# A decoder block in split fp32: scaled activations made by VectorE in wide pieces, w_up's halves added a tick later, the keys' transposes four ticks later

## The chip, the cores and the metric

The kernel runs on one core of a Trainium2 chip, as one program. The metric is the device time of one execution in microseconds (us). The engines are TensorE (PE in the profile; PEld is its weight load), VectorE (DVE), ScalarE (ACT), GpSimd (POOL) and SyncE (SP), which starts most of the transfers. Each engine works through its own instructions in the order in which the program holds them and waits on semaphores for what others produce.

## The reference

One layer of a decoder, in float32, for 256 tokens of width 1024:

```
h = rms_norm(x, norm_mix_g);  proj = h @ w_in            # u | q | k | v, 512 each
q, k = rope(rms_norm(q)), rope(rms_norm(k))              # 8 heads of 64
x = x + concat(pool_mixer(u), attention(q, k, v)) @ w_out
h = rms_norm(x, norm_xattn_g)
x = x + cross_attention(h, rms_norm(mem)) @ w_xo         # 4 heads of 256, 256 memory rows
h = rms_norm(x, norm_ffn_g)
up = causal_conv3(h @ w_up) + conv_b                     # 2 x 2816 channels
x = x + (silu(gate) * val) @ w_down                      # 2816 -> 1024
```

The outputs are the 256 x 1024 values of the last x.

## The kernel before

**Products in three passes.** TensorE takes operands in a rounded format (fp32r). Each fp32 operand is split into a high part h (rounded) and a low part l (the rest), and a product is h·h + h·l + l·h. Activations are split once per stage: ScalarE rounds (`part_h`, L253 and L255), VectorE subtracts (`part_l`, L259 and L261). A split activation tile lies as [h | l], 512 columns for 256 tokens.

**Weights.** All weights stream from HBM as chunks of 1 MB (`raw`), each two units of 1024 columns. For each unit ScalarE makes `wh` (L194) and VectorE `wl` (L205); `need(u)` puts both into the program at the point at which a unit is first asked for, some units ahead of its use.

**Matmuls.** The in-projection is made by `a_chunk` (L378 to L390), with the weights as the moving operand: for each of 8 blocks of the width, h and l of two token tiles against `wh`, then h against `wl`. All later projections are made by `b_tile` with `both` (L276 to L282): for each block of 128 inputs one matmul of `wh` against [h | l] (512 columns; L278 or L282) and one of `wl` against h (256 columns; L279 or L281). The halves of the bank, h and l products, are added afterwards. L278 and L279 are the first pair of a tile, so L278 marks where a tile opens.

**The order of the work.** The matmuls are written in their order. All other work (norms, rotations, transposes, softmax, the convolution) is written as generators, the jobs. `tick()`, called after every second block, advances each open job by one step, and the numbers in the WAIT lists say how many ticks a job lets pass before its next step. So these numbers fix where each instruction stands on each engine; at run time only semaphores decide when it runs.

**Keys and queries.** `rope` and `qk_job` rotate and normalize them: products with the rotation tables, a sum (L432), a sum of squares, an inverse root on GpSimd, for the keys a product with it (L453), then eight transposes on TensorE (L460) and copies by ScalarE. The in-projection of u runs beside this. WAIT_QK[1] is the wait before the keys' transposes, WAIT_QK[0] that before the queries'.

**w_up.** 22 pairs of tiles, gate and value, of 8 blocks each. The norm's factor for each token (`r2b`, made at L910 by `r2_job`) is not there when the stage begins. The first three pairs (i < SCALED) use unscaled activations and their result is multiplied by r2b (L934). The others use `hs2`: the same activations with the factor in them. Eight GpSimd products (L920) make them, eight ScalarE activations round them, eight VectorE operations (L261) subtract. After a pair's second tile `up_job` (L924 to L956) runs: for both halves ScalarE copies the l part out of the bank (L928) and VectorE adds the h part (L929); ScalarE starts the convolution (y, L938), VectorE adds its two other taps (L945, four operations), ScalarE takes silu (L949), VectorE multiplies gate and value (L951), and the result is rounded and subtracted (L253, L259) into `act`, one of 22 blocks of w_down's input.

**w_down.** Eight tiles of 22 blocks, L984 to L990. Before a block is used, `act_tile` lets that pair's job run to its end. Each tile's halves are added to the residual by two VectorE additions (L989), and the result goes out by DMA.

**The head.** Twenty small matmuls (L351) run while the first weights and tokens arrive; `first_splits` splits the activations and the first weights, block by block.

Of the kernel before, what the change touches and what calls it, by code (L numbers as in the profile page):

```python
# [18 lines left out]
S = 256  # L19
KT = D // P  # L20
# [19 lines left out]
WAIT_MEAN = [0]  # L40
WAIT_STAT = [2, 14, 8, 0, 0, 30]
WAIT_ROPE = [6, 6, 0]
WAIT_QK = [12, 12, 8, 25, 0, 2]
WAIT_V = [2, 10]
WAIT_MEM = [2, 2]
WAIT_SCORE = [5, 4, 0, 9, 1, 6]
# [3 lines left out]
WAIT_R1 = [6]  # L50
WAIT_X = [3, 0, 0, 0, 10, 0, 6, 13, 8]
WAIT_VALUE = [32]
WAIT_R2 = [6, 6, 1, 1, 0]
WAIT_LOW = [2]
WAIT_UP = [6, 2, 5, 7, 9, 8]
SCALED = 3
# [21 lines left out]
def block_kernel(ctx: ExitStack, tc: tile.TileContext, wpack: bass.AP, xpack: bass.AP, scal: bass.AP,  # L78
# [56 lines left out]
    def wait(n):  # L135
        for _ in range(n):
            yield
# [113 lines left out]
    def part_h(h, src, scale=None):  # L251
        if scale is None:
            act.copy(h, src)  # L253
        else:
            act.activation(h, src, AF.Copy, scale=scale)  # L255
# [12 lines left out]
    def three(o, stat, mov, start, stop):  # L268
# [2 lines left out]
        pe.matmul(o, stat[0], mov[1], start=False, stop=False)  # L271
        pe.matmul(o, stat[1], mov[0], start=False, stop=stop)  # L272

    def both(b, stat, mov, start, stop):

        n = mov.shape[1] // 2  # L276
        if start:
            pe.matmul(b, stat[0], mov, start=True, stop=False)  # L278
            pe.matmul(b[:, 0:n], stat[1], mov[:, 0:n], start=False, stop=False)  # L279
        else:  # L280
            pe.matmul(b[:, 0:n], stat[1], mov[:, 0:n], start=False, stop=False)  # L281
            pe.matmul(b, stat[0], mov, start=False, stop=stop)  # L282

    def col(t, c):
        return t[:, c:c + 1]
# [80 lines left out]

    def first_splits():
        for k in range(KT):
            part_h(xgv[0][:, k], resid[:, k], col(sc, C_GMIX + k))
            part_l(xgv[1][:, k], resid[:, k], xgv[0][:, k], col(sc, C_GMIX + k))  # L370
            r = slice(k % 2 * 512, k % 2 * 512 + 512)
            split_h(k // 2, r, dve.tensor_copy if k == 0 else act.copy)
            split_l(k // 2, r)
        next_split[0] = FIRST

# [2 lines left out]
    def a_chunk(u0, actv, bk):  # L378

        for k in range(KT):  # L380
            w = need(u0 + k // 2)
            wv = [t[:, (k % 2) * 512:(k % 2) * 512 + 512] for t in w]
            a = [[t[:, k, tt * P:(tt + 1) * P] for t in actv[:2]] for tt in range(TT)]
            for tt in range(TT):
                pe.matmul(bk[tt], a[tt][0], wv[0], start=k == 0, stop=False)  # L385
                pe.matmul(bk[tt], a[tt][1], wv[0], start=False, stop=False)  # L386
            tick()
            for tt in range(TT):
                pe.matmul(bk[tt], a[tt][0], wv[1], start=False, stop=k == KT - 1)  # L389
            tick()  # L390
# [330 lines left out]

    def b_tile(u0, f, blocks, b, mov):

        for k in range(blocks):
            i = f * blocks + k
            w = need(u0 + i // 8)
            wv = [t[:, (i % 8) * P:(i % 8 + 1) * P] for t in w]
            both(b, wv, mov(k), k == 0, k == blocks - 1)
            halves[0] += 1
            if halves[0] % 2 == 0 and k < blocks - 1:  # L730
                tick()
# [168 lines left out]
    def r2_job():  # L900

        yield from wait(WAIT_R2[0])
        v2 = yield from row_mean(acc2, "2")
        r2 = rsqrt(v2, TT, True)
        yield from wait(WAIT_R2[1])
        b = bank()
        for tt in range(TT):
            pe.matmul(b[:, tt * P:(tt + 1) * P], col(r2, tt).to_broadcast([P, P]), ident, start=True, stop=True)
        yield from wait(WAIT_R2[2])
        dve.tensor_copy(r2b, b[:, 0:S])  # L910
        r2_ready.append(True)
        yield from wait(WAIT_R2[3])
        prev = None
        for k in range(KT + 1):
            if prev is not None:
                part_h(hs2[0][:, k - 1], prev, col(sc, C_GFFN + k - 1))
                part_l(hs2[1][:, k - 1], prev, hs2[0][:, k - 1], col(sc, C_GFFN + k - 1))
            if k < KT:
                t = t1(f"hs{k}")
                pool.tensor_tensor(t, resid[:, k], r2b, op=ALU.mult)  # L920
                prev = t
            yield from wait(WAIT_R2[4])

    def up_job(i, bs, scaled):  # L924
        src = t2(f"up{i}")
        for g in range(2):
            half = src[:, g * S:(g + 1) * S]
            act.copy(half, bs[g][:, S:])  # L928
            dve.tensor_tensor(half, bs[g][:, 0:S], half, op=ALU.add)  # L929
        if not scaled:  # L930
            while not r2_ready:
                yield
            src2 = src.rearrange("p (g s) -> p g s", g=2)
            dve.tensor_tensor(src2, src2, r2b[:, None, :].to_broadcast([P, 2, S]), op=ALU.mult)  # L934
        y = t2(f"y{i}")
        for g in range(2):
            f = i + g * NFF
            act.activation(y[:, g * S:(g + 1) * S], src[:, g * S:(g + 1) * S], AF.Identity, bias=col(sc, C_CB + f),  # L938
                           scale=col(sc, C_CW + 2 * 2 * NFF + f))
        yield from wait(WAIT_UP[1])  # L940
        for j in (1, 2):
            for g in range(2):
                f = i + g * NFF
                uu, yy = src[:, g * S:(g + 1) * S], y[:, g * S:(g + 1) * S]
                dve.scalar_tensor_tensor(yy[:, j:], uu[:, :S - j], col(sc, C_CW + (2 - j) * 2 * NFF + f), yy[:, j:],  # L945
                                         op0=ALU.mult, op1=ALU.add)
        yield from wait(WAIT_UP[2])
        sg = t2(f"sg{i}")
        act.activation(sg[:, 0:S], y[:, 0:S], AF.Silu)  # L949
        yield from wait(WAIT_UP[3])  # L950
        dve.tensor_tensor(sg[:, S:], sg[:, 0:S], y[:, S:], op=ALU.mult)  # L951
        yield from wait(WAIT_UP[4])
        h, l = (t[:, i % 8] for t in acts[i // 8][:2])
        part_h(h, sg[:, S:])
        yield from wait(WAIT_UP[5])
        part_l(l, sg[:, S:], h)  # L956
# [2 lines left out]
    jobs_up = []  # L959
    look[0] = LOOKS[10]  # L960
    for i in range(NFF):
        bs = [bank(), bank()]
        if i == 0:
            hs2 = tiles(pair("hs2"), KT, S)
            job_r2.append(go(r2_job()))
        scaled = i >= SCALED
        hv = hs2 if scaled else h2
        if i == SCALED:
            finish(job_r2[0])
        for g in range(2):  # L970
            b_tile(58, 2 * i + g, KT, bs[g], lambda k: hv[2][:, k])
            if g == 0:
                tick()
        if i % 8 == 0:
            acts.append(tiles(pair(f"act{i // 8}"), KT, S))
        jobs_up.append(go(up_job(i, bs, scaled)))
        tick()

    def act_tile(k):
# [2 lines left out]

    look[0] = LOOKS[11]
    for f in range(KT):  # L984
        b = bank()
        b_tile(102, f, NFF, b, act_tile)
        o = t2(f"o{f}")[:, 0:S]
        for z, add in enumerate((resid[:, f], o)):
            dve.tensor_tensor(o, b[:, z * S:(z + 1) * S], add, op=ALU.add)  # L989
        nc.sync.dma_start(out[:, f], o)  # L990

# [98 lines left out]
```

## Time and profile before

| what | us |
|---|---|
| median of 3 runs | 391.47 |
| lowest, highest run | 390.37, 392.4 |
| the profiled execution: its time | 390.8 |
| the profiled execution: span from the first to the last instruction | 389.0 |
| PE busy | 381.3 (98% of the span) |
| DVE busy | 313.3 (81%) |
| ACT busy | 248.2 (64%) |
| POOL busy | 77.1 (20%) |

The span leaves out 1.8 us of the profiled execution's time that lie around it. Rows of a timeline give the start, the length, the engine, the line, the operation and out<-in; `x4` joins four neighbours, and a bracket gives the idle time before them and what ended it. The length of an instruction is longer than the distance to its neighbour's start, since neighbours overlap. Waits are given as total, times, longest. The granted TensorE clock is 1.000 over the whole execution.

### The profile page before, as it was taken

Reading aid. Unit: us, or ns where it says so; the run is one execution under the profiler, and the core shown is the slowest. Engines: PE = TensorE matmul, PEld = TensorE weight load, DVE = VectorE, ACT = ScalarE, POOL = GpSimd, SP = SyncE. Lnnn points to the kernel's source line nnn. Section 1 sums busy time; section 2 is a strip of 40 time slices with the busy share of each in tenths; the row PEclk is TensorE's granted clock in tenths of the full one; section 3 lists DMA queues with packets and bytes.
Section 4 is the critical chain, followed back from the end, with each engine's and each line's share of the span. In section 5 each row is a group of like instructions: output and inputs, shape, how many; then the busy total and the mean of one; then the engine's idle time right before and its main releaser. Section 6 shows DMA issues by size and latency. Waiting matters only on the chain.

```text
span 389.0 us, 5984 instructions
## 1 busy us (share of the span) xinstructions
PE 381.3 (98%) x2178; PEld 328.7 (84%) x2178; DVE 313.3 (81%) x562; ACT 248.2 (64%) x475; POOL 77.1 (20%) x160
## 2 busy tenths in 40 slices
PE   8999899999999999999999999999999999999995
PEld 8888688888888988898888878888888888888884
DVE  4769899978879859678978989999999998654460
ACT  5775797977557747745655678778877777442210
POOL 0272786142832122100325100000000000000000
PEclk9999999999999999999999999999999999999999
DMA  8985381453505624363535055555655554364400
GB/s 281 423 329 192 134 305 67 176 211 110 199 19 216 217 108 190 135 217 109 189 125 231 1 155 204 196 211 209 218 216 202 184 191 181 124 241 166 186 19 21
DMA packets 12269, 69.14 MB, mean 178 GB/s; under 512 B 1360, under 2 KB 2768, under 8 KB 4688
## 3 DMA queue, kind: packets, MB, share of 16 engines
q1 hardware_dynamic: 11952, 68.24, 47.5%
q10 hardware_dynamic: 288, 0.52, 0.4%
q8 instruction: 17, 0.28, 0.3%
q14 instruction: 12, 0.10, 0.1%
HBM read 67.71 MB, written 1.05 MB: 177 GB/s over the span
## 4 chain that ended last, share of the span: by engine, by line
PE 79%; DVE 9%; DMA 3%; ACT 3%; issue 2%; POOL 2%; SPq 0%; DVEq 0%
PE bank L282 34%; PE bank L281 17%; PE bank L385 5%; PE bank L386 5%; PE bank L389 5%; PE bank L278 4%; DVE wl L205 3%; PE bank L279 2%; DMA raw<-wpack 2%; DVE hs L261 2%; DMA sc<-xpack 1%; PE bank L272 1%; PE bank L271 1%; PE bank L270 1%; ACT wh L194 1%
## 5 line engine op out<-in xcount | busy, mean ns | idle before, releaser
L205 DVE TENSOR_TENSOR wl<-raw,wh 128x1024 fp32r<-128x1024 f32 (+1 forms) x126 | 149.3, 1202 | 3.1 <-ACT wh L194 3.1
L194 ACT CAST wh<-raw 128x1024 fp32r<-128x1024 f32 (+1 forms) x125 | 123.6, 1022 | 36.0 <-DMA raw<-wpack 35.0
L282 PE MATMUL bank<-hs,wh 128*128 128x512 f32 x266 | 94.8, 396 | 0.0
L281 PE MATMUL bank<-hs,wl 128*128 128x256 f32 x266 | 74.2, 279 | 0.0
L282 PE MATMUL bank<-act,wh 128*128 128x512 f32 x168 | 59.6, 398 | 0.0
L282 PEld LDWEIGHTS bank<-hs,wh 128*128 128x128 f32 x266 | 49.9, 188 | 10.3
L281 PEld LDWEIGHTS bank<-hs,wl 128*128 128x128 f32 x266 | 50.1, 189 | 1.6
L281 PE MATMUL bank<-act,wl 128*128 128x256 f32 x168 | 47.1, 281 | 0.0
L938 ACT ACTIVATE y<-up,sc 128x256 f32<-128x256 f32 x44 | 24.1, 595 | 27.0 <-DVE up L929 19.7
L282 PEld LDWEIGHTS bank<-act,wh 128*128 128x128 f32 x168 | 31.6, 188 | 7.4
L945 DVE SCALAR_TENSOR_TENSOR y<-up,sc,y 128x255 f32<-128x255 f32 (+1 forms) x88 | 36.6, 477 | 0.3 <-ACT y L938 0.3
L282 PE MATMUL bank<-h,wh 128*128 128x512 f32 x98 | 35.1, 396 | 0.0
L281 PEld LDWEIGHTS bank<-act,wl 128*128 128x128 f32 x168 | 31.7, 189 | 0.3
L281 PE MATMUL bank<-h,wl 128*128 128x256 f32 x98 | 27.6, 281 | 0.0
L989 DVE TENSOR_TENSOR o<-bank,sc 128x256 f32<-128x256 f32 x8 | 3.4, 425 | 29.4 <-PE bank L282 29.4
L385 PE MATMUL bank<-wh,mg 128*128 128x512 f32 x64 | 26.1, 408 | 0.0
L385 PE MATMUL bank<-wh,xg 128*128 128x512 f32 x64 | 26.0, 406 | 0.0
L386 PE MATMUL bank<-wh,xg 128*128 128x512 f32 x64 | 25.4, 397 | 0.0
L386 PE MATMUL bank<-wh,mg 128*128 128x512 f32 x64 | 25.1, 392 | 0.0
L747 POOL TENSOR_TENSOR h_acc<-h_sq,h_acc 128x256 f32<-128x256 f32 x14 | 13.4, 956 | 43.3 <-ACT h_sq L746 43.1
L282 PEld LDWEIGHTS bank<-h,wh 128*128 128x128 f32 x98 | 18.4, 188 | 3.6
L255 ACT ACTIVATE h<-sc 128x256 fp32r<-128x256 f32 x16 | 8.2, 511 | 20.5 <-DVE sc L739 20.4
(256 smaller groups left out, 770.1 us busy)
## 6 DMA issues: line engine op xcount, KB each, us to landing
raw<-wpack SPq DMA_DIRECT2D x59, 1024.0 KB, 4.8
raw<-wpack SPq DMA_DIRECT2D x4, 512.0 KB, 7.8
mraw<-memT SPq DMA_DIRECT2D x4, 256.0 KB, 6.8
out<-o SPq DMA_DIRECT2D x8, 128.0 KB, 1.9
raw<-wpack ACTq DMA_DIRECT2D x2, 256.0 KB, 3.5
raw<-wpack SPq DMA_DIRECT2D x2, 256.0 KB, 4.8
sc<-xpack SPq DMA_DIRECT2D x1, 512.0 KB, 6.4
tab<-table SPq DMA_DIRECT2D x1, 480.0 KB, 9.1
```

Source lines behind the costliest of these rows:

```text
L194: copy(split[u][0][:, r], unit(u)[:, r])
L205: dve.tensor_tensor(l[:, r], unit(u)[:, r], h[:, r].bitcast(F32), op=ALU.subtract)
L255: act.activation(h, src, AF.Copy, scale=scale)
L278: pe.matmul(b, stat[0], mov, start=True, stop=False)
L281: pe.matmul(b[:, 0:n], stat[1], mov[:, 0:n], start=False, stop=False)
L282: pe.matmul(b, stat[0], mov, start=False, stop=stop)
L385: pe.matmul(bk[tt], a[tt][0], wv[0], start=k == 0, stop=False)
L386: pe.matmul(bk[tt], a[tt][1], wv[0], start=False, stop=False)
L389: pe.matmul(bk[tt], a[tt][0], wv[1], start=False, stop=k == KT - 1)
L747: pool.tensor_tensor(acc, sq, acc, op=ALU.add)
L938: act.activation(y[:, g * S:(g + 1) * S], src[:, g * S:(g + 1) * S], AF.Identity, bias=col(sc, C_CB + f), scale=col(sc, C_CW + 2 * 2 * NFF ...
L945: dve.scalar_tensor_tensor(yy[:, j:], uu[:, :S - j], col(sc, C_CW + (2 - j) * 2 * NFF + f), yy[:, j:], op0=ALU.mult, op1=ALU.add)
```

## The change

Six things are changed.

- `r2_job`: VectorE makes the scaled activations (eight operations with gain and r2b at once, L922) instead of GpSimd; ScalarE rounds them in four pieces of 512 columns and VectorE subtracts in four pieces (L259). The waits there go from 1, 0 to 0, 1.
- The adding of a pair's halves leaves `up_job`. A new generator `up_half` is started after each tile: ScalarE copies at once, VectorE adds two ticks later (L932). `up_job` waits two ticks before its first step.
- WAIT_QK[1], ahead of the keys' transposes, goes from 12 to 16.
- `first_splits`: the cast of the first weights stands ahead of the first activations' subtraction.
- `a_chunk`: the h products of both token tiles come first, then the l products of both.
- The last tile of w_down uses `three` (three matmuls of 256 columns a block, summed in one bank half) and one addition.

```diff
-WAIT_QK = [12, 12, 8, 25, 0, 2]
+WAIT_QK = [12, 16, 8, 25, 0, 2]
...
-WAIT_R2 = [6, 6, 1, 1, 0]
+WAIT_R2 = [6, 6, 1, 0, 1]
...
+    def halves_of(t):
+        return [t[:, 0:S], t[:, S:]]
...
             part_h(xgv[0][:, k], resid[:, k], col(sc, C_GMIX + k))
+            split_h(k // 2, r, dve.tensor_copy if k == 0 else act.copy)
             part_l(xgv[1][:, k], resid[:, k], xgv[0][:, k], col(sc, C_GMIX + k))
-            split_h(k // 2, r, dve.tensor_copy if k == 0 else act.copy)
...
                 pe.matmul(bk[tt], a[tt][0], wv[0], start=k == 0, stop=False)
+            for tt in range(TT):
                 pe.matmul(bk[tt], a[tt][1], wv[0], start=False, stop=False)
...
+        product = both if b.shape[1] > S else three
...
-            both(b, wv, mov(k), k == 0, k == blocks - 1)
+            product(b, wv, mov(k), k == 0, k == blocks - 1)
...
-        prev = None
-        for k in range(KT + 1):
-            if prev is not None:
-                part_h(hs2[0][:, k - 1], prev, col(sc, C_GFFN + k - 1))
-                part_l(hs2[1][:, k - 1], prev, hs2[0][:, k - 1], col(sc, C_GFFN + k - 1))
-            if k < KT:
-                t = t1(f"hs{k}")
-                pool.tensor_tensor(t, resid[:, k], r2b, op=ALU.mult)
-                prev = t
-            yield from wait(WAIT_R2[4])
-
-    def up_job(i, bs, scaled):
-        src = t2(f"up{i}")
-        for g in range(2):
-            half = src[:, g * S:(g + 1) * S]
-            act.copy(half, bs[g][:, S:])
-            dve.tensor_tensor(half, bs[g][:, 0:S], half, op=ALU.add)
+        ts = []
+        for j in range(KT // 2):
+            ts.append(t2(f"hs{j}").rearrange("p (k s) -> p k s", k=2))
+            for k in range(2):
+                dve.scalar_tensor_tensor(ts[j][:, k], resid[:, 2 * j + k], col(sc, C_GFFN + 2 * j + k), r2b,
+                                         op0=ALU.mult, op1=ALU.mult)
+            part_h(hs2[0][:, 2 * j:2 * j + 2], ts[j])
+        yield from wait(WAIT_R2[4])
+        for j in range(KT // 2):
+            part_l(hs2[1][:, 2 * j:2 * j + 2], ts[j], hs2[0][:, 2 * j:2 * j + 2])
+
+    def up_half(o, b):
+        act.copy(o, b[:, S:])
+        yield from wait(WAIT_LOW[0])
+        dve.tensor_tensor(o, b[:, 0:S], o, op=ALU.add)
+
+    def up_job(i, src, scaled):
+        yield from wait(WAIT_LOW[0])
...
-        bs = [bank(), bank()]
+        up = t2(f"up{i}")
...
-            b_tile(58, 2 * i + g, KT, bs[g], lambda k: hv[2][:, k])
+            b = bank()
+            b_tile(58, 2 * i + g, KT, b, lambda k: hv[2][:, k])
+            go(up_half(up[:, g * S:(g + 1) * S], b))
...
-        jobs_up.append(go(up_job(i, bs, scaled)))
+        jobs_up.append(go(up_job(i, up, scaled)))
...
-        b = bank()
-        b_tile(102, f, NFF, b, act_tile)
+        last = f == KT - 1
+        b = bank()[:, 0:S] if last else bank()
+        b_tile(102, f, NFF, b, (lambda k: halves_of(act_tile(k))) if last else act_tile)
...
-        for z, add in enumerate((resid[:, f], o)):
+        for z, add in enumerate((resid[:, f], o)[:1 if last else 2]):
```

The order on VectorE in the steady part of w_up, before: the work of pair 5 (`up5`, `y5`), with older pairs' products (`sg4`) and subtractions (from `sg2`) between. Rows give line, operation, out<-in and the shape.

```order
L929 TENSOR_TENSOR up5_2650<-bank99_2596,up5_2650 128x256
L929 TENSOR_TENSOR up5_2650<-bank100_2597,up5_2650 128x256
L205 TENSOR_TENSOR wl74_2662<-raw37_2502,wh74_2625 128x1024
L945 SCALAR_TENSOR_TENSOR y5_2655<-up5_2650,sc_75,y5_2655 128x255 x2
L945 SCALAR_TENSOR_TENSOR y5_2655<-up5_2650,sc_75,y5_2655 128x254 x2
L205 TENSOR_TENSOR wl75_2688<-raw37_2502,wh75_2660 128x1024
L951 TENSOR_TENSOR sg4_2640<-sg4_2640,y4_2593 128x256
L259 TENSOR_TENSOR act0_2311<-sg2_2517,act0_2311 128x256
```

The same pair on VectorE in the changed kernel, where the line numbers are 3 to 6 higher (L932 the add, L951 the y-operations, L957 the product of gate and value):

```order
L932 TENSOR_TENSOR up5_2580<-bank99_2581,up5_2580 128x256
L957 TENSOR_TENSOR sg3_2578<-sg3_2578,y3_2530 128x256
L259 TENSOR_TENSOR act0_2315<-sg1_2456,act0_2315 128x256
L205 TENSOR_TENSOR wl74_2646<-raw37_2492,wh74_2615 128x1024
L932 TENSOR_TENSOR up5_2580<-bank100_2612,up5_2580 128x256
L951 SCALAR_TENSOR_TENSOR y5_2653<-up5_2580,sc_75,y5_2653 128x255 x2
L951 SCALAR_TENSOR_TENSOR y5_2653<-up5_2580,sc_75,y5_2653 128x254 x2
L205 TENSOR_TENSOR wl75_2678<-raw37_2492,wh75_2644 128x1024
```

The instructions of a pair are the same ones. The first half's add has moved up, ahead of the wl of unit 74; the second half's add has moved behind that wl and stands right ahead of the y-operations.

The order on TensorE at the keys' transposes (L460, `m1k`), before, in the in-projection of u:

```order
L389 MATMUL bank_523<-wl_398,xg 128x512
L389 MATMUL bank_524<-wl_398,xg 128x512
L460 MATMUL bank_534<-tab,m1k_271 128x128 x4
L460 MATMUL bank_539<-tab,m1k_276 128x128 x4
L385 MATMUL bank_523<-wh_343,xg 128x512
L386 MATMUL bank_523<-wh_343,xg 128x512
```

And TensorE's rows in the changed kernel from there to the queries' transposes (L464, `m1q`):

```order
L393 MATMUL bank_524<-wl_416,xg 128x512
L464 MATMUL bank_561<-tab,m1k_271 128x128 x4
L464 MATMUL bank_566<-tab,m1k_276 128x128 x4
L388 MATMUL bank_523<-wh_396,xg 128x512
L388 MATMUL bank_524<-wh_396,xg 128x512
L390 MATMUL bank_523<-wh_396,xg 128x512
L390 MATMUL bank_524<-wh_396,xg 128x512
L393 MATMUL bank_523<-wl_416,xg 128x512
L393 MATMUL bank_524<-wl_416,xg 128x512
L464 MATMUL bank_584<-tab,m1q_384 128x128 x4
L464 MATMUL bank_589<-tab,m1q_389 128x128 x4
```

The keys' transposes have moved behind 12 matmuls. The queries' are where they were, so that 6 matmuls lie between the two, where before there were 18.

The order on VectorE behind r2b, before, from the last subtractions of the scaled activations on:

```order
L261 SCALAR_TENSOR_TENSOR hs2_2245<-hs6_2385,sc_75,hs2_2245 128x256
L261 SCALAR_TENSOR_TENSOR hs2_2245<-hs7_2389,sc_75,hs2_2245 128x256
L945 SCALAR_TENSOR_TENSOR y0_2354<-up0_2312,sc_75,y0_2354 128x255 x2
L945 SCALAR_TENSOR_TENSOR y0_2354<-up0_2312,sc_75,y0_2354 128x254 x2
L929 TENSOR_TENSOR up1_2405<-bank90_2317,up1_2405 128x256
L929 TENSOR_TENSOR up1_2405<-bank91_2318,up1_2405 128x256
L934 TENSOR_TENSOR up1_2405<-up1_2405,r2b_2242 128x512
L205 TENSOR_TENSOR wl66_2418<-raw33_2246,wh66_2344 128x1024
```

And VectorE in the changed kernel, from the last products on:

```order
L922 SCALAR_TENSOR_TENSOR hs3_2367<-sc_75,r2b_2242 128x256 x2
L940 TENSOR_TENSOR up0_2243<-up0_2243,r2b_2242 128x512
L932 TENSOR_TENSOR up1_2316<-bank90_2317,up1_2316 128x256
L259 TENSOR_TENSOR hs2_2244<-hs0_2355,hs2_2244 128x2x256
L259 TENSOR_TENSOR hs2_2244<-hs1_2359,hs2_2244 128x2x256
L259 TENSOR_TENSOR hs2_2244<-hs2_2363,hs2_2244 128x2x256
L259 TENSOR_TENSOR hs2_2244<-hs3_2367,hs2_2244 128x2x256
L951 SCALAR_TENSOR_TENSOR y0_2372<-up0_2243,sc_75,y0_2372 128x255 x2
L951 SCALAR_TENSOR_TENSOR y0_2372<-up0_2243,sc_75,y0_2372 128x254 x2
L205 TENSOR_TENSOR wl66_2401<-raw33_2246,wh66_2346 128x1024
```

Eight products and four wide subtractions stand where eight subtractions stood; the wl of unit 66 now comes ahead of the second half's add of pair 1 and its r2b product, which follow it.

More of the change, by code (lines that the diff above doesn't have):

```diff
@@ L368, in first_splits @@
         for k in range(KT):
+            r = slice(k % 2 * 512, k % 2 * 512 + 512)
             part_h(xgv[0][:, k], resid[:, k], col(sc, C_GMIX + k))
+            split_h(k // 2, r, dve.tensor_copy if k == 0 else act.copy)
             part_l(xgv[1][:, k], resid[:, k], xgv[0][:, k], col(sc, C_GMIX + k))
-            r = slice(k % 2 * 512, k % 2 * 512 + 512)
-            split_h(k // 2, r, dve.tensor_copy if k == 0 else act.copy)
             split_l(k // 2, r)
```

## The prediction

> **What bounds the kernel now.** I read the page first, then TensorE's waits.
>
> ```profile
> PE 381.3 (98%) x2178; PEld 328.7 (84%) x2178; DVE 313.3 (81%) x562; ACT 248.2 (64%) x475; POOL 77.1 (20%) x160
> ```
>
> ```profile
> PE bank L460 <- DVE m1k L453: 1.4, 1, 1.4
> ...
> PE bank L279 <- DVE wl L205: 1.0, 1, 1.0
> ```
>
> TensorE is busy for 381.3 of 389.0 us, so the kernel ends when the matmuls end, and the only time to be had is its few stalls. Two of them are named: the keys' transposes (L460) wait for VectorE, and so does a w_up tile (L279). A share over the whole span hides what a stage can bear, though, so next I asked for VectorE's busy time in w_up alone.
>
> ```profile
> 227.50:324.20 96.70, 96.50 (x551) 83.86 (x552) 96.70 (x188) 77.53 (x151) 0.00 (x0) 1.00 0.55 197
> 227.50:329.20 101.70, 101.50 (x580) 88.21 (x581) 101.26 (x200) 80.81 (x158) 0.00 (x0) 1.00 0.55 198
> ```
>
> The columns are the length, then PE, PEld, DVE, ACT and POOL. VectorE is busy for all of 96.70 us: it is behind TensorE throughout w_up, working off a backlog. Whether it wins or loses ground is read from its timeline over one pair of tiles (start, length; starts of neighbours give the cost of each), against the starts of TensorE's tiles.
>
> ```profile
> 256.87 0.74 DVE L929 TENSOR_TENSOR up<-bank,up 128x256 f32<-128x256 f32 x2
> 257.53 1.21 DVE L205 TENSOR_TENSOR wl<-raw,wh 128x1024 fp32r<-128x1024 f32 x1
> 258.66 1.66 DVE L945 SCALAR_TENSOR_TENSOR y<-up,sc,y 128x255 f32<-128x255 f32 x4
> 260.24 1.22 DVE L205 TENSOR_TENSOR wl<-raw,wh 128x1024 fp32r<-128x1024 f32 x1
> 261.38 0.42 DVE L951 TENSOR_TENSOR sg<-sg,y 128x256 f32<-128x256 f32 x1
> 261.71 0.42 DVE L259 TENSOR_TENSOR act<-sg,act 128x256 fp32r<-128x256 f32 x1
> 262.05 0.74 DVE L929 TENSOR_TENSOR up<-bank,up 128x256 f32<-128x256 f32 x2
> ```
>
> ```profile
> L278 PE MATMUL bank<-hs,wh x38: 388/397/402, 214.8 to 320.1; 128*128 128x512 f32 x38
> ```
>
> ```profile
> 322.22 0.28 PE L281 MATMUL bank<-hs,wl 128*128 128x256 f32 x1
> 322.34 0.40 PE L282 MATMUL bank<-hs,wh 128*128 128x512 f32 x1
> ...
> 322.92 0.40 PE L278 MATMUL bank<-act,wh 128*128 128x512 f32 x1
> ...
> 330.55 0.39 PE L278 MATMUL bank<-act,wh 128*128 128x512 f32 x1
> ```
>
> VectorE repeats after 262.05 - 256.87 = 5.18 us. L278 opens a tile: the last of w_up opens at 320.1 and w_down at 322.92, so a tile is 2.80 us and a pair 5.60. VectorE gains 0.42 us per pair. The 38 tiles with scaled activations hold 105.3 us between their first and last start, 37 x 2.80 would be 103.6: 1.7 us are stalls. How little is spare at the end shows in VectorE's last work for w_up:
>
> ```profile
> 324.24 0.75 DVE L929 TENSOR_TENSOR up<-bank,up 128x256 f32<-128x256 f32 x2
> 325.33 1.77 DVE L945 SCALAR_TENSOR_TENSOR y<-up,sc,y 128x255 f32<-128x255 f32 x4 [0.34 <-ACT y L938]
> ...
> 328.02 1.09 DVE L259 TENSOR_TENSOR act<-sg,act 128x256 fp32r<-128x256 f32 x3
> ```
>
> The last of the 22 activations is ready at 329.11. The first w_down tile takes 330.55 - 322.92 = 7.63 us for 22 blocks, so it needs that one at about 330.2. The margin is 1.1 us.
>
> **The change part by part.** *Scaled activations.* Before, after r2b:
>
> ```profile
> 208.08 0.42 DVE L910 COPY r2b<-bank 128x256 f32<-128x256 f32 x1
> 208.53 0.69 DVE L934 TENSOR_TENSOR up<-up,r2b 128x512 f32<-128x512 f32 x1
> 210.79 5.92 DVE L261 SCALAR_TENSOR_TENSOR hs<-hs,sc,hs 128x256 fp32r<-128x256 f32 x8 [1.56 <-ACT hs L255]
> 216.64 1.65 DVE L945 SCALAR_TENSOR_TENSOR y<-up,sc,y 128x255 f32<-128x255 f32 x4
> ...
> 219.60 1.22 DVE L205 TENSOR_TENSOR wl<-raw,wh 128x1024 fp32r<-128x1024 f32 x1
> ...
> 226.43 1.22 DVE L205 TENSOR_TENSOR wl<-raw,wh 128x1024 fp32r<-128x1024 f32 x1
> ```
>
> ```profile
> L261 DVE SCALAR_TENSOR_TENSOR hs<-hs,sc,hs x8: 470/955/964, 210.8 to 216.2; 128x256 fp32r<-128x256 f32 x8
> ```
>
> ```profile
> 226.36 0.39 PE L278 MATMUL bank<-hs,wh 128*128 128x512 f32 x1
> 227.70 0.38 PE L279 MATMUL bank<-hs,wl 128*128 128x256 f32 x1 [0.96 <-DVE wl L205]
> ```
>
> VectorE idles 1.56 us, then pays 0.955 for subtractions that take 0.470 when GpSimd isn't multiplying beside them. It gets to w_up's weights late: the wl of unit 68 starts at 226.43, and TensorE's second matmul comes 1.34 us after the first instead of 0.23. After: from 208.53 eight products at the y-operations' pace of (260.24 - 258.66)/4 = 0.395 end at 211.7; the r2b product (0.61) at 212.3, one add (0.33) at 212.6, four subtractions of 512 columns at 0.61 each at 215.1.
>
> ```profile
> L259 DVE TENSOR_TENSOR ox<-bank,ox 128x512 fp32r<-128x512 f32 x4 | 2.8, 692 | 2.4 <-ACT ox L253 2.4
> ```
>
> (0.692 is the length; the next instruction starts 0.08 before the end, as behind a wl, 1.21 long with starts 1.13 apart: 0.61.) TensorE opens its first scaled tile at 214.8 and takes a block every 0.35 us, and the subtractions go by two blocks per 0.61, so they stay ahead. Then four y-operations (1.58), a wl (1.13, at 216.7 instead of 219.60), an add and an r2b product (0.94), an idle of 0.75 for ScalarE's y (1.09 from an add's start to the y-operation, shown below; the r2b product is 0.27 longer than an add and itself takes 0.61), y-operations (1.58), a wl and an add (1.46): the wl of unit 68 starts at 222.5, or at 223.0 if ScalarE's cast is late. I take 223.0, 3.4 us earlier. Of that, 0.94 is only put off (an add and an r2b product of pair 2 now stand behind it), so 2.5 us are won for the backlog, and the 1.7 us of stalls go.
>
> *Halves one tick later.* This moves instructions on VectorE: the second half's add now stands right in front of its pair's y-operations, with the wl ahead of it. Before, that wl (257.53, 1.13 us) hid the way from the add through ScalarE's y and back. The last pair has no wl there, and shows the price uncovered: the add starts at 324.24, the y-operation at 325.33, 1.09 us. The first half's y is ready early now, so after the add (0.33) one y-operation (0.395) can run; then VectorE, which works in order, stands for 1.09 - 0.33 - 0.395 = 0.36 us, and the adds, the wl and the products behind it stand too. Between bounds of 0 (all covered) and 0.76 (nothing between) I take 0.36, by that row. VectorE's period becomes 5.54 against TensorE's 5.60, and the backlog is hardly worked off any more: pairs 3 to 20, 18 x 0.36 = 6.5 us.
>
> The last activation is then ready at 329.11 - 2.5 + 6.5 = 333.1. TensorE, freed of 1.7 us, opens w_down at 321.2 and wants it at 328.5. So it stands at blocks 17 to 21, and opens the second tile 0.4 after 333.1, at 333.5 instead of 330.55: **+2.95**. The stalls saved earlier are in that number: they only lengthen the wait at its end.
>
> *Keys' transposes.* Their place moves past 12 matmuls; the queries' transposes stay.
>
> ```profile
> 40.40 0.61 PE L389 MATMUL bank<-wl,xg 128*128 128x512 f32 x2
> 42.46 1.32 PE L460 MATMUL bank<-tab,m1k 128*128 128x128 f32 x8 [1.44 <-DVE m1k L453]
> ```
>
> ```profile
> 47.17 0.68 DVE L432 TENSOR_TENSOR m1q<-m1q,m2q 128x512 f32<-128x512 f32 x1
> ```
>
> ```profile
> 47.75 1.03 PE L460 MATMUL bank<-tab,m1q 128*128 128x128 f32 x8
> ```
>
> TensorE could start them at 40.86 and loses 1.6 us. 12 matmuls at 0.23 put them at 43.6, behind the keys' product: the wait goes. But then TensorE reaches the queries at 46.15, and their sum (L432) ends only at 47.86, by a VectorE chain that never waited for TensorE. Four transposes run on the first half, four after 47.9: the end is 48.4 instead of 48.54. **-0.2**, where 1.6 was removed.
>
> *First cast first, and the h products of both token tiles first.* The first product starts straight behind the warm-up matmuls:
>
> ```profile
> 4.21 1.49 PE L351 MATMUL bank<-idle 128*128 128x128 f32 x6
> 5.36 0.77 PE L385 MATMUL bank<-wh,xg 128*128 128x512 f32 x1
> 5.93 0.63 PE L386 MATMUL bank<-wh,xg 128*128 128x512 f32 x1
> 6.35 0.63 PE L385 MATMUL bank<-wh,xg 128*128 128x512 f32 x1
> ```
>
> An earlier cast can't bring it forward: the warm-up covers it. Without that cover, one subtraction (0.4) would be at stake. The same matmuls in another order are taken at **0**.
>
> *Last w_down tile.* Three 256-column matmuls a block replace one of 256 and one of 512 columns: by 322.22 to 322.34, 0.117 to 0.12 each, 22 x 3 of them 7.7 to 7.9 for 7.63 to 7.7 before, so 0 to +0.2; I take +0.1. At the end one add goes:
>
> ```profile
> 385.12 0.42 DVE L989 TENSOR_TENSOR o<-bank,sc 128x256 f32<-128x256 f32 x1 [5.74 <-PE bank L282]
> 385.57 0.42 DVE L989 TENSOR_TENSOR o<-bank,o 128x256 f32<-128x256 f32 x1
> ```
>
> 385.57 - 385.12 = 0.45 on the path with nothing beside it: **-0.35** together.
>
> Sum: the profiled execution took 390.8 (span 389.0). 390.8 - 0.2 + 2.95 - 0.35 = 393.2. The runs shown have a median of 391.47, 0.7 above it, from 390.37 to 392.4; I forecast 393.6, between 393.2 and 393.9.
>
> **The rivals.** *VectorE keeps up (faster).* If the idle of 0.36 is nearly covered, the last activation is in time and the savings stand. It decides at 333.1 - 328.5 = 4.6 us: the idle would have to be under (6.5 - 4.6)/18 = 0.1 per pair. For it: 5.54 is under 5.60 still. Against: the 0.34 in the last pair's row. Time: 390.8 - 1.7 - 0.2 - 0.35 = 388.6, by the median 389.2.
>
> *Part of the idle (no change).* With 0.2 to 0.25 a pair, the last activation comes at 330.2 to 331.1, the second tile at 330.6 to 331.5, up to +0.9: 390.3 to 391.2, by the median up to 391.9.
>
> *The clock falls (slower still).* From about 327 to 333 TensorE would have two waits near 2 us and only five blocks of work. The granted clock is 1.00 in every row shown, and the wait of 1.6 us before 42.46 didn't lower it; but at the head neighbours start 0.42 apart (5.93, 6.35) where they later take 0.23, so a cold TensorE exists here. A cold stretch loses 1 - 0.23/0.42 = 0.45 of its length; the head's rows are cold for 2 us at least (4.21 to 6.35), and I take 2 to 8 us: 0.9 to 3.6 on top, 394.1 to 396.8, by the median up to 397.5. It decides by how TensorE's five blocks are spread, which no row shows. [...]
>
> **How the numbers follow.** Forecast 0.55, its own range 392.3 to 394.9 (0.05 a pair either way is 0.9, the start of unit 68 another 0.4); keeping up 0.16; part of the idle 0.16; clock 0.13. The range is 390.1 to 395.9: it holds the forecast and the partial case, and leaves out most of the case that keeps up and half of the clock. About 0.5% (2 us) is what a measurement of this kernel tells from no change, so the bounds are 389.5 and 393.4. Faster: most of keeping up, 0.14. Slower: the clock's 0.13 and the upper 0.33 of the forecast, 0.46. The same: the rest, 0.40.
>
> **What would show it.** In the changed trace: VectorE idle before L951 (the y-operations), about 0.36 us in each of 18 pairs, released by ScalarE's y; TensorE waiting for act's subtraction (L259) in the first w_down tile, 4 to 5 us in all, and the second tile at about 333.5; no wait at the keys' transposes, and one of 1.5 us at the queries'; no wait for wl near 227; one add at the end. I am wrong if VectorE shows no idle in w_up, or if w_down's first tile runs without a wait.

## The result, and the profile after

| | before | changed |
|---|---|---|
| median, 4 runs each | 391.43 us | 395.89 us |
| lowest, highest | 390.37, 392.4 | 395.05, 396.57 |
| the profiled execution: time, span | 390.8, 389.0 | 396.22, 394.2 |
| granted TensorE clock over the span | 1.000 | 0.991 |

The changed kernel is slower: ratio 1.0114, with a 95% interval of 1.008 to 1.0147. The forecast was 393.6 in a range of 390.1 to 395.9; what came is the forecast's mechanism with the rival of the falling clock on top of it, and the median is inside the range by 0.01 us only. The median before is a mixture: of the 41 executions of that kernel that the experiments recorded, 16 had a mean granted clock of 0.996 or less and were 1.6 us longer at the median (392.16 for 390.54), while the profiled one had 1.000, so the medians differ by 4.46 us and the profiled executions by 5.42.

TensorE's waits in the changed kernel (total, times, longest), and VectorE's from 227.6 us on:

```profile
PE bank L285 <- DVE act L259: 4.5, 2, 2.3
PE bank L464 <- DVE m1q L436: 1.8, 2, 1.3
```

```profile
DVE y L951 <- ACT y L944: 5.3, 19, 0.3
```

The waits for the keys and for wl are gone. In their place are two at the queries and two, 4.5 us together, for the activations in w_down's first tile. VectorE had one idle before its y-operations; now it has 19. One pair of the steady part, VectorE's timeline in the changed kernel:

```profile
256.32 0.42 DVE L932 TENSOR_TENSOR up<-bank,up 128x256 f32<-128x256 f32 x1
256.66 0.42 DVE L957 TENSOR_TENSOR sg<-sg,y 128x256 f32<-128x256 f32 x1
256.99 0.42 DVE L259 TENSOR_TENSOR act<-sg,act 128x256 fp32r<-128x256 f32 x1
257.32 1.22 DVE L205 TENSOR_TENSOR wl<-raw,wh 128x1024 fp32r<-128x1024 f32 x1
258.46 0.42 DVE L932 TENSOR_TENSOR up<-bank,up 128x256 f32<-128x256 f32 x1
258.79 0.48 DVE L951 SCALAR_TENSOR_TENSOR y<-up,sc,y 128x255 f32<-128x255 f32 x1
259.55 1.27 DVE L951 SCALAR_TENSOR_TENSOR y<-up,sc,y 128x255 f32<-128x255 f32 x3 [0.28 <-ACT y L944]
260.74 1.22 DVE L205 TENSOR_TENSOR wl<-raw,wh 128x1024 fp32r<-128x1024 f32 x1
261.87 0.42 DVE L932 TENSOR_TENSOR up<-bank,up 128x256 f32<-128x256 f32 x1
```

The second add starts at 258.46 and the second y-operation at 259.55, 1.09 us later, with one y-operation between them. The bracket says 0.28 idle, but neighbours overlap by 0.08, so the slot lost is 259.55 - 258.79 - 0.395 = 0.36. The period is 261.87 - 256.32 = 5.55 us. Nothing here looks wrong on its own: VectorE is still busy for 91.98 of the 96.70 us from 227.50 to 324.20. Its debt comes due at the change of stages. TensorE's tiles in w_down (each L281 opens one), and VectorE's last work for w_up:

```profile
329.61 0.50 PE L285 MATMUL bank<-act,wh 128*128 128x512 f32 x1 [2.19 <-DVE act L259]
...
332.56 0.80 PE L285 MATMUL bank<-act,wh 128*128 128x512 f32 x1 [2.32 <-DVE act L259]
...
335.10 0.63 PE L281 MATMUL bank<-act,wh 128*128 128x512 f32 x1
...
343.99 0.40 PE L281 MATMUL bank<-act,wh 128*128 128x512 f32 x1
```

```profile
332.75 1.09 DVE L259 TENSOR_TENSOR act<-sg,act 128x256 fp32r<-128x256 f32 x3
```

The last activation is ready at 333.84 instead of 329.11, and the second tile opens at 335.10 instead of 330.55: +4.55. That tile then takes 8.89 us. Before, it took 7.77, by the opening of the third:

```profile
330.55 0.39 PE L278 MATMUL bank<-act,wh 128*128 128x512 f32 x1
338.32 0.39 PE L278 MATMUL bank<-act,wh 128*128 128x512 f32 x1
```

The windows around it give TensorE's busy time and, behind the bracket, the granted clock:

```profile
327.00:331.00 4.00, 1.04 (x5) 1.00 0.37 109
331.00:337.60 6.60, 5.04 (x15) 0.50 0.32 130
```

From 331.0 to 337.6 the clock is at half; the window from 337 to 338 us has 0.58, so the stretch ends at about 337.8. The end, in the changed kernel and in the kernel before, is the issue of the last output:

```profile
390.81 0.42 DVE L998 TENSOR_TENSOR o<-bank,sc 128x256 f32<-128x256 f32 x1 [5.89 <-PE bank L272]
391.26 0.33 SPq L999 DMA_DIRECT2D out<-o  x1
```

```profile
386.03 0.33 SPq L990 DMA_DIRECT2D out<-o  x1
```

From the third tile to it: 391.26 - 343.99 = 47.27, before 386.03 - 338.32 = 47.71, so 0.44 won. 4.55 + 1.12 - 0.44 = 5.23, which is the difference of these two issues: all of the loss lies between 321 and 344 us.

### The profile page after: what moved, and what is told of

Read it like the earlier page. It is cut to its first block, busy times and chain, and to the rows that moved or that the text cites. A ratio compares the mean times of both kernels' runs of the same rounds, so it can differ in the third digit from the quotient of the medians.

```text
span 394.2 us, 6036 instructions
## 1 busy us (share of the span) xinstructions
PE 383.2 (97%) x2200; PEld 331.7 (84%) x2200; DVE 314.3 (80%) x565; ACT 247.2 (63%) x471; POOL 70.1 (18%) x152
## 4 chain that ended last, share of the span: by engine, by line
PE 52%; DVE 33%; ACT 6%; DMA 3%; issue 3%; POOL 2%; SPq 0%; DVEq 0%
PE bank L285 18%; DVE wl L205 15%; PE bank L284 9%; DVE y L951 6%; PE bank L388 4%; PE bank L390 4%; PE bank L393 4%; DVE up L932 4%; ACT y L944 3%; DMA raw<-wpack 2%; PE bank L281 2%; PE bank L272 2%; PE bank L271 2%; PE bank L270 2%; DVE act L259 2%
## 5 line engine op out<-in xcount | busy, mean ns | idle before, releaser
L194 ACT CAST wh<-raw 128x1024 fp32r<-128x1024 f32 (+1 forms) x125 | 125.7, 1024 | 37.7 <-DMA raw<-wpack 37.3
L285 PE MATMUL bank<-act,wh 128*128 128x512 f32 x147 | 54.2, 409 | 4.5 <-DVE act L259 4.5
L944 ACT ACTIVATE y<-up,sc 128x256 f32<-128x256 f32 x44 | 26.2, 602 | 31.0 <-DVE up L932 25.7
L951 DVE SCALAR_TENSOR_TENSOR y<-up,sc,y 128x255 f32<-128x255 f32 (+1 forms) x88 | 38.4, 479 | 6.3 <-ACT y L944 6.3
L284 PE MATMUL bank<-act,wl 128*128 128x256 f32 x147 | 42.0, 286 | 0.0
L285 PEld LDWEIGHTS bank<-act,wh 128*128 128x128 f32 x147 | 28.6, 194 | 11.8 <-DVE act L259 5.3
L284 PEld LDWEIGHTS bank<-act,wl 128*128 128x128 f32 x147 | 28.7, 195 | 0.4
L388 PE MATMUL bank<-wh,mg 128*128 128x512 f32 x64 | 20.9, 408 | 0.0
L388 PE MATMUL bank<-wh,xg 128*128 128x512 f32 x64 | 20.7, 405 | 0.0
L390 PE MATMUL bank<-wh,xg 128*128 128x512 f32 x64 | 20.0, 393 | 0.0
L285 PE MATMUL bank<-cat,wh 128*128 128x512 f32 x56 | 20.0, 394 | 0.0
```

The lines of the kernel that those rows point to most:

```text
L194: copy(split[u][0][:, r], unit(u)[:, r])
```

## The experiments

Theory: the later add opens the way from the add through ScalarE to the y-operations, VectorE loses 0.36 us a pair, the debt stops TensorE at the first tile of w_down, and the idle there halves the clock. Rivals: the scaled activations overload VectorE; splitting the adds costs by itself; the loss grows pair by pair rather than from a margin; the half clock costs nothing, since those blocks wait anyway. Each ratio is to the kernel before, run on the same chip.

**The halves together again, the other five edits kept.**

```diff
-            go(up_half(up[:, g * S:(g + 1) * S], b))
...
-    def up_job(i, src, scaled):
-        yield from wait(WAIT_LOW[0])
+    def up_job(i, bs, scaled):
+        src = t2(f"up{i}")
+        for g in range(2):
+            half = src[:, g * S:(g + 1) * S]
+            act.copy(half, bs[g][:, S:])
+            dve.tensor_tensor(half, bs[g][:, 0:S], half, op=ALU.add)
```

> The changed kernel with the two halves of a pair added together again, both ahead of a wl (the other five edits stay). Theory (the way from the second half's add to the y-operations lies open, 0.36 us a pair, and the clock's fall follows from it): no idle of VectorE before the y-operations of pairs 3 to 20, no wait in the first w_down tile, granted clock 1.000, 388.6 to 389.6 us. Rival (the scaled activations on VectorE are what overloads it): the wait in the first w_down tile stays at 3 to 5 us, 394 to 396 us.

Measured: 388.24 us, ratio 0.9925 (0.9903 to 0.9947), a little under the range expected. VectorE's waits from 227.6 us on that are for ScalarE, and the opening of w_down's second tile:

```profile
DVE y L950 <- ACT y L943: 0.3, 1, 0.3
```

```profile
328.26 0.39 PE L281 MATMUL bank<-act,wh 128*128 128x512 f32 x1
```

One idle, that of the last pair, and no wait of TensorE for an activation. So one of six edits makes the loss, and the other five together are a gain. The rival of the scaled activations falls.

**The halves alone, on the kernel before.** This part of the change and nothing else:

```diff
+    def up_half(o, b):
+        act.copy(o, b[:, S:])
+        yield from wait(WAIT_LOW[0])
+        dve.tensor_tensor(o, b[:, 0:S], o, op=ALU.add)
...
+    def up_job(i, src, scaled):
+        yield from wait(WAIT_LOW[0])
```

> The kernel before with the later, separate adding of the halves as its only edit. Theory: the idle of 0.36 us a pair is there, and the late start behind r2b (GpSimd's products) too, so VectorE is later at the end of w_up than in the changed kernel by 0.5 to 2.5 us; second w_down tile at 335.5 to 337.5, clock below 1.000, 396.5 to 398.5 us. Rival (the scaled activations are the cost): within 1 us of the kernel before, 390.5 to 392.5.

Measured: 398.01 us, ratio 1.0184 (1.0143 to 1.0225). TensorE's waits, and the opening of the second tile:

```profile
PE bank L282 <- DVE act L259: 4.2, 2, 2.2
```

```profile
336.06 0.63 PE L278 MATMUL bank<-act,wh 128*128 128x512 f32 x1
```

Two such waits again, on a kernel that has GpSimd's products still: the edit is enough by itself. By the medians it is worse without the gain of the others, though the two intervals overlap a little. The first wait's end, and TensorE's window with its granted clock:

```profile
330.57 0.79 PE L282 MATMUL bank<-act,wh 128*128 128x512 f32 x1 [2.21 <-DVE act L259]
```

```profile
330.00:335.00 5.00, 2.49 (x7) 0.54 0.53 210
```

If the clock there is 0.50 from its fall on, a mean of 0.54 over these 5 us means half clock for 4.6 of them, from about 330.4: by this estimate it fell 2.0 us into the wait that began at 328.36, before TensorE was back at work.

**Spare work in the waits.** The changed kernel with:

```diff
+    FILL = {17: 10, 18: 10}
+
+    def fill(n):
+        b = bank() if n else None
+        for _ in range(n):
+            pe.matmul(b, acts[1][0][:, 0, 0:P], acts[1][2][:, 0], start=True, stop=True)
+
     def act_tile(k):
         finish(jobs_up[k])
+        fill(FILL.pop(k, 0))
```

> The changed kernel with ten spare matmuls of 512 columns on TensorE ahead of block 17 and ten ahead of block 18 of the first w_down tile, into a bank that nothing reads, so that TensorE is busy while it waits for VectorE. VectorE's work is untouched. Theory (about 2 us of the loss is the half clock from 331 to 337.6, because TensorE was idle): granted clock 1.000, matmuls of the second tile 0.23 and 0.12 apart, 1.6 to 2.3 us under the changed kernel: 393.5 to 394.3. Rival (the half clock only slows blocks that wait for VectorE anyway): within 0.5 us of the changed kernel's 395.9.

Measured: 394.38 us, ratio 1.0086 (1.0054 to 1.0118). The windows of TensorE (length, busy, clock), and the second tile's opening:

```profile
330.00:335.00 5.00, 4.90 (x24) 1.00 0.47 197
335.00:340.00 5.00, 5.00 (x30) 1.00 0.34 103
```

```profile
334.14 0.39 PE L281 MATMUL bank<-act,wh 128*128 128x512 f32 x1
```

The clock stays at 1.00 and the time falls by 1.5 us, though twenty useless matmuls were added and VectorE is as late as before. That is a little under the 1.6 to 2.3 expected, but in the profiled executions the spans differ by 394.2 - 392.3 = 1.9. One of the four executions, the longest at 395.39, had a mean granted clock of 0.996, the others 0.999 and above. The half clock is a cost of its own. The rest, to the 388.24 of the halves together, is VectorE's lateness: the second tile opens 5.88 us later here (334.14 for 328.26), and the spans differ by 5.9 (392.3 for 386.4).

**One tick instead of two.**

```diff
-WAIT_LOW = [2]
+WAIT_LOW = [2]; WAIT_HALF = [1, 1]
...
     def up_half(o, b):
         act.copy(o, b[:, S:])
-        yield from wait(WAIT_LOW[0])
+        yield from wait(WAIT_HALF[0])
...
     def up_job(i, src, scaled):
-        yield from wait(WAIT_LOW[0])
+        yield from wait(WAIT_HALF[1])
```

> The changed kernel with the halves' adds and the pair's job one tick after the tile instead of two: the adds stay separate, but both stand ahead of a wl, and that wl is between the second add and the y-operations again. Theory (it is what stands between the add and the y-operations): as with the halves together, no idle in the pairs, no wait in w_down's first tile, clock 1.000, 388.6 to 389.6 us. Rival (adding the halves separately costs by itself, through ScalarE's order or the banks): above 392 us.

Measured: 388.83 us, ratio 0.9939 (0.9915 to 0.9962). VectorE, one pair:

```profile
259.63 0.44 DVE L932 TENSOR_TENSOR up<-bank,up 128x256 f32<-128x256 f32 x1
259.96 1.24 DVE L205 TENSOR_TENSOR wl<-raw,wh 128x1024 fp32r<-128x1024 f32 x1
261.09 1.69 DVE L951 SCALAR_TENSOR_TENSOR y<-up,sc,y 128x255 f32<-128x255 f32 x4
```

The adds are as separate as in the changed kernel, but a wl fills the way, and VectorE's one idle is that of the last pair. One tick or two, at these two places, decides between 388.8 and 395.9. Separate adds by themselves cost nothing that the intervals of this run and of the halves together tell apart.

**Half the pairs.** One tick in even pairs, two in odd ones, in both places:

```diff
-WAIT_LOW = [2]
+WAIT_LOW = [2]; WAIT_HALF = [1, 2]
...
-    def up_half(o, b):
+    def up_half(o, b, n):
...
-        yield from wait(WAIT_LOW[0])
+        yield from wait(n)
...
-        yield from wait(WAIT_LOW[0])
+        yield from wait(WAIT_HALF[i % 2])
...
-            go(up_half(up[:, g * S:(g + 1) * S], b))
+            go(up_half(up[:, g * S:(g + 1) * S], b, WAIT_HALF[i % 2]))
```

> The changed kernel with one tick instead of two in the even pairs only, so that 9 or 10 of the pairs leave the way from the add to the y-operations open. Theory (a margin is used up first, then the rest shows, and the clock falls only with a long idle): idle of VectorE in about 10 pairs; its last work for w_up 3.2 us earlier than in the changed kernel, at about 330.6; one or two short waits in w_down's first tile, 1.5 to 2.3 us together; granted clock 1.000; 390.0 to 391.2 us. Rival (each pair costs its share of the loss): midway between 388.8 and 395.9, 392.0 to 392.7.

Measured: 390.31 us, ratio 0.9978 (0.9959 to 0.9997). TensorE's wait in w_down's first tile, and VectorE's idles:

```profile
PE bank L285 <- DVE act L259: 1.3, 1, 1.3
```

```profile
DVE y L951 <- ACT y L944: 2.8, 10, 0.3
```

Ten idles instead of 19, one wait of 1.3 us instead of 4.5, the clock at 1.00 in that stretch. Half the cause makes 1.5 us over the kernel with none (388.83), while the whole makes 7.1: a margin is used up first, and the clock, 0.50 behind the changed kernel's waits of 2.19 and 2.32 us, stayed at 1.00 behind this one of 1.27. VectorE's last work for w_up ended at 329.38, earlier than the 330.6 expected, and the wait was shorter than expected; this execution opened w_down at 320.29 instead of 321.24, which is most of the difference.

**The keys' transposes alone, on the kernel before.**

```diff
-WAIT_QK = [12, 12, 8, 25, 0, 2]
+WAIT_QK = [12, 16, 8, 25, 0, 2]
```

> The kernel before with the keys' transposes 4 ticks later as its only edit. Theory (the wait moves on to the queries' transposes, which have the same place and wait for VectorE's sums): no wait at the keys, 1.2 to 2.2 us at the queries in two pieces, the second of them 0.5 whatever the rest does; time within 0.5 us of the kernel before. Rival (the wait of 1.6 us goes): 1.2 to 1.7 us faster.

Measured: 390.4 us, ratio 0.9979 (0.9961 to 0.9997). TensorE's waits:

```profile
PE bank L460 <- DVE m1q L432: 1.0, 2, 0.5
PE bank L279 <- DVE wl L205: 1.0, 1, 1.0
```

The wait has moved to the queries, in two pieces as expected, though 1.0 us together is under the 1.2 expected. By the medians the gain is 0.85 us, more than the 0.5 that the theory allowed and less than the rival's 1.2, with an interval from 0.1 to 1.5. The profiled executions give the theory's size: the product behind the queries' transposes starts at 48.05 instead of 48.54, 0.49 earlier, and the spans are 388.5 and 389.0. What the medians have beyond that goes with the clock: 2 of these 12 executions had a mean granted clock of 0.996 or less, 16 of 41 before.

**The scaled activations alone, on the kernel before.** The part of the change in `r2_job` with its waits; these lines of it put the products on VectorE:

```diff
-                pool.tensor_tensor(t, resid[:, k], r2b, op=ALU.mult)
+                dve.scalar_tensor_tensor(ts[j][:, k], resid[:, 2 * j + k], col(sc, C_GFFN + 2 * j + k), r2b,
+                                         op0=ALU.mult, op1=ALU.mult)
```

> The kernel before with the scaled activations by VectorE in wide pieces as its only edit. Theory (VectorE comes to the weights of w_up 3 us earlier and TensorE's 1.6 us of waits for wl go): no wait for wl near 227, no wait in w_down's first tile, 389.4 to 390.2 us. Rival (eight products more on an engine that is behind make the backlog longer): waits stay or grow, 391 us and above.

Measured: 389.17 us, ratio 0.9955 (0.9933 to 0.9976), just better than the 389.4 to 390.2 expected. Of TensorE's waits this remains, and none for wl or an activation:

```profile
PE bank L460 <- DVE m1k L453: 1.6, 1, 1.6
PE bank L351 <- DVE idle L348: 1.1, 1, 1.1
```

Eight products more on the busiest helper still make it earlier, because it no longer idles for GpSimd's first product (1.56 us before) nor subtracts beside its others (eight subtractions before, 0.955 us each at the median, 0.470 the shortest, and 5.92 together; four wide ones take 2.48 together in the changed kernel).

**The queries' transposes too.** The kernel with one tick, and:

```diff
-WAIT_QK = [12, 16, 8, 25, 0, 2]
+WAIT_QK = [15, 16, 8, 25, 0, 2]
```

> The changed kernel with the halves one tick after the tile, and the queries' transposes moved past 10 more matmuls as well (15 ticks instead of 12). Theory: with both transposes moved the wait for VectorE's chain goes and nothing else is late; no wait for m1q; 0.7 to 1.8 us under the kernel with the halves at one tick (388.8): 387.0 to 388.1. Rival (the wait moves on once more, to the scores that take the queries): a wait at L536 or L540, within 0.4 us of 388.8.

Measured: 387.89 us, ratio 0.9911 (0.9887 to 0.9935): the fastest of all, 3.4 us under the kernel before. TensorE's waits:

```profile
PE bank L536 <- ACT qkT L468: 0.7, 1, 0.7
PE bank L388 <- DVE pf L652: 0.4, 1, 0.4
PE bank L282 <- DVE wl L205: 0.2, 1, 0.2
```

No wait for m1q, but part of it comes back: the scores (L536) wait for the queries' copies, which they don't in the kernel with one tick. The product that waits for VectorE (L388) stands 21 us later, at 72.08, and that it goes back to the moved queries is not shown. Both theories have a share. The 0.9 us under the kernel with one tick are no more than the two intervals leave open.

**Only one wait filled.** The spare matmuls ahead of block 17 alone, and in a second kernel ahead of block 18 alone:

```diff
-    FILL = {17: 10, 18: 10}
+    FILL = {17: 10}
```

> The changed kernel with ten spare matmuls ahead of block 17 only, so that only the second wait of about 2.3 us in w_down's first tile is idle. Theory (the clock falls on the low share of work over several us that the two waits make together, not on one wait of 2.3 us): granted clock 1.000, 393.6 to 395.0 us, as with both waits filled. Rival (one wait of 2.3 us is enough): half clock behind it, 395.5 us and above.

> The changed kernel with ten spare matmuls ahead of block 18 only, so that only the first wait of about 2.3 us is idle. Theory (the two waits together): granted clock 1.000, 393.6 to 395.0 us. Rival (one wait is enough): half clock from about 331 on, 395.5 us and above.

Measured: 394.99 us, ratio 1.0119 (1.009 to 1.0149), and 394.52 us, ratio 1.0107 (1.0078 to 1.0136). The first of them, the wait left and the clock behind it:

```profile
331.95 0.50 PE L285 MATMUL bank<-act,wh 128*128 128x512 f32 x1 [2.33 <-DVE act L259]
```

```profile
332.00:333.50 1.50, 1.45 (x7) 1.00 0.08 33
333.50:337.00 3.50, 3.50 (x13) 0.51 0.11 37
```

And the second:

```profile
329.07 0.50 PE L285 MATMUL bank<-act,wh 128*128 128x512 f32 x1 [2.12 <-DVE act L259]
```

```profile
329.00:330.40 1.40, 1.33 (x6) 1.00 0.63 205
330.40:333.80 3.40, 3.40 (x11) 0.50 0.53 224
```

Here my theory failed and the rival held as to the clock: one wait was enough, of 2.33 us in the first and 2.12 us in the second. The clock fell 1.6 and 1.3 us after TensorE was back at work, and stayed at half for about 3.4 us, half as long as the 6.8 in the changed kernel. The times alone would not have shown it: both lie in the range of the theory, below the rival's 395.5, since one such stretch costs less than two.

## Why the prediction was right, point by point

- **What bounds.** Right: a backlog on VectorE that a share over the span doesn't show, and a margin of 1.1 us at the end of w_up.
- **The idle of 0.36 us a pair.** Right: 0.36 in the rows, period 5.55 for the 5.54 predicted. Taking it from the one pair of the kernel before that had the way open was enough. The halves together, one tick and half the pairs show that it is the cause.
- **The lateness it makes.** Right in kind, a little too small. The last activation was to be ready at 333.1 and came at 333.84. From the wl of unit 68 to it, VectorE took 110.71 us (223.13 to 333.84) for 102.68 before (226.43 to 329.11), 8.0 more where 0.94 + 6.5 = 7.44 was predicted. Pair 2 has an idle too, which I had not counted: its y-operations start at 226.09, 0.75 behind the start of a product of 0.33, so 0.4 of the 0.6; the other 0.2 stays open. With the clock kept up by spare work, the second tile opened at 334.14, in an execution that opened w_down 0.13 earlier (321.11 for 321.24). So the changed kernel would have opened it at 334.27 without the clock, 3.72 later than before. 0.14 of that came from the queries, below, which leaves 3.6 for the 2.95 of the sum.
- **Scaled activations.** Right. VectorE's timeline behind r2b in the changed kernel:

```profile
208.67 3.25 DVE L922 SCALAR_TENSOR_TENSOR hs<-sc,r2b 128x256 f32<-128x256 f32 x8
...
212.78 2.48 DVE L259 TENSOR_TENSOR hs<-hs,hs 128x512 fp32r<-128x512 f32 x4
...
216.76 1.22 DVE L205 TENSOR_TENSOR wl<-raw,wh 128x1024 fp32r<-128x1024 f32 x1
...
223.13 1.23 DVE L205 TENSOR_TENSOR wl<-raw,wh 128x1024 fp32r<-128x1024 f32 x1 [0.18 <-ACT wh L194]
```

  The products, the subtractions and the two wl stand within 0.2 us of where the sum had put them (208.53, 212.6, 216.7, 223.0). Alone the edit is worth 2.1 us by the medians and 1.9 by the profiled executions (390.8 and 388.91).
- **The keys' transposes.** The wait moved to the queries as predicted. TensorE and VectorE in the changed kernel:

```profile
43.36 1.03 PE L464 MATMUL bank<-tab,m1k 128*128 128x128 f32 x8
...
47.07 0.66 PE L464 MATMUL bank<-tab,m1q 128*128 128x128 f32 x4 [1.29 <-DVE m1q L436]
48.27 0.66 PE L464 MATMUL bank<-tab,m1q 128*128 128x128 f32 x4 [0.54 <-DVE m1q L436]
```

```profile
47.53 0.68 DVE L436 TENSOR_TENSOR m1q<-m1q,m2q 128x512 f32<-128x512 f32 x1
```

  The queries' sum started at 47.53 instead of 47.17, the product behind the transposes started at 48.68 instead of 48.54, and in this execution the term was +0.14 instead of -0.2 (the prediction's own 48.4 for 48.54 makes -0.14). The same chain started its sum at 46.90 in the kernel with the keys alone, and at 47.10 with the halves together, 46.62 with one tick and 47.40 with both waits filled, whose programs are the changed one up to w_up. So it moves by some tenths from execution to execution, and since TensorE waits for its end, so does the time. Why it moves was not tried.
- **First cast, order of the a_chunk products.** Put at 0; no run took them alone, so this stays argued only.
- **Last tile.** From the opening of the third tile to the last output 0.44 us were won where 0.35 was the sum.
- **The clock.** It was a rival at 0.13 and happened. Its price was predicted at 0.9 to 3.6 us. It cost 1.95: the second tile opened 335.10 - 334.27 = 0.83 later, and took 8.89 - 7.77 = 1.12 more. The failed step is the chance: it took two waits near 2 us to leave the clock alone, most likely, and no row of the kernel before showed a wait of that length. TensorE's longest wait there, before 42.46, is 1.44 us by its bracket (1.6 is the time lost) and left the clock at 1.00. The runs with one wait filled show half clock behind single waits of 2.12 and 2.33 us. In the traces the waits of 1.6 us (at the keys, in the scaled activations alone) and 1.27 us (half the pairs) did leave it at 1.00. The price per stretch was right: at half clock a block took 0.64 us (334.03 to 334.67) instead of 0.35, so 0.45 of the stretch is lost. Its length, 6.8 us, lies within the 2 to 8 us taken, of which the 8 was my guess, with no row behind it. The head, from which the prediction took the price, has the spacing of half clock (0.42 between 5.93 and 6.35; 0.42 between 335.10 and 335.52 at 0.50). But the trace's clock records begin at 7.22 us in the kernel before and at 6.74 in the changed one, so the granted clock at the head is not shown; the 1.00 printed there is no reading.

So the profiled execution's 396.22 us come out of the sum's 393.2: + 0.63 of lateness that was under-counted (3.58 for 2.95), + 0.34 at the queries (+0.14 for -0.2), + 1.95 of the clock, - 0.09 at the end (0.44 for 0.35), and 0.2 more around the span (2.0 for 1.8).

The mechanism was right, but that the number lay in the range was luck. The forecast's own range was 392.3 to 394.9; the clock's 1.95, the 0.63 of lateness and the 0.34 at the queries were not in it, and together they reached the upper bound of 395.9: two of the four executions, 396.22 and 396.57, lie above it.

## What to carry to other kernels

On an engine that works in order and is nearly full, look at what stands between the start of a round trip to another engine and its return: moving one independent instruction out of that place costs its cover in every turn of the loop (here a wl of 1.13 us, and 0.36 us a pair), and the bill comes at the next stage (here 4.5 us of waits in w_down). Compare the engine's period with the bound's, not its share of the span, and add up turns until the margin is gone. Ask of a wait of TensorE whether it costs more than its length: here the clock was at 0.50 for about 3.4 us behind single waits of 2.12 and 2.33 us, and at 1.00 behind waits of 1.27 and 1.6 us.

## What the runs showed of the hardware

The granted clock fell to 0.50 behind single idles of 2.12 and 2.33 us, and where two idles followed each other (2.19 and 2.32 us in the changed kernel, 2.21 and 1.94 us with the halves alone). The delay differed. With one idle filled and one left, the fall came 3.4 to 3.9 us after the idle's start, 1.3 to 1.6 us after work had begun again. In the changed kernel it came 3.6 us after the first idle's start (327.42 to 331.0), in the second idle. With the halves alone it came, by the estimate from the mean of 0.54, 2.0 us after the first idle's start, while TensorE still stood. What sets the delay was not tried. The clock stayed at half for about 3.4 us behind one idle (330.4 to 333.8, 333.5 to 337.0) and 6.8 us behind two (331.0 to 337.8). With TensorE kept at spare work it stayed at 1.00 in the profiled execution.

In the traces, idles of 1.27 us (half the pairs) and 1.6 us (at the keys, in the scaled activations alone) left the clock at 1.00. That they always do is not shown. Of the executions of the kernel before and of the scaled activations alone, which keep the wait at the keys (1.44 and 1.6 us in the traces), 20 of 50 had a mean granted clock of 0.996 or less. Of those with the halves together, one tick, half the pairs, the keys alone, the queries too and both waits filled, which don't have it, 4 of 43 had. (The other kernels' traces show the fall in w_down.) No trace of such an execution was kept, so where the clock fell in them is open. By an estimate from the figures above, 3.4 us at half clock lose 0.45 x 3.4 = 1.5 us; these executions of the kernel before are 1.6 us longer at the median.
